# The end of a large matmul: leaving the last bank to the end and summing it in two halves

## Chip, cores and metric

One core of a Trainium2 chip. Kernels are compared only within the same rounds. The metric is the device time of one execution in microseconds (us), medians over several runs.

## The reference

```python
def setup_inputs():
    m, k, n = 4096, 4096, 4096
    return {
        "a": np.random.randn(m, k).astype(np.float32),
        "b": np.random.randn(k, n).astype(np.float32),
        "alpha": np.float32(0.01),
    }

def reference(a, b, alpha):
    x = np.matmul(a, b)
    return np.where(x > 0, x, alpha * x)
```

## The kernel before

The kernel works in bf16. It goes through the output in regions of 512 rows by 1024 columns: four row blocks (`mt`) times two column halves (`nt`), which are eight sums of 128 x 512 fp32, one in each of the eight PSUM banks. k is passed in four quarters (`u`) of eight steps of 128 (`c`). The parts that the change touches:

```python
    psum_pool = ctx.enter_context(tc.tile_pool(name="psum", bufs=8, space=bass.MemoryType.PSUM))
    o_pool = ctx.enter_context(tc.tile_pool(name="oo", bufs=2))
    # ... cut ...
    def mm(ps, mb, h, pi, u, mt, nt, c, first, last):
        rows = slice(mt * P, (mt + 1) * P)
        t = at[mb, h, u]
        nc.tensor.matmul(
            ps,
            plain(t)[:, c, rows] if (mb, h, u) == (0, 0, 0) else t[:, c // 2, rows, c % 2],
            bt[pi, u][:, c, nt * NT:(nt + 1) * NT],
            start=first,
            stop=last,
        )
    # ... cut: the first two regions, loads, transposes ...
    for r in range(HALVES, len(regions)):
        mb, h, pi, n = regions[r]
        banks = new_banks()
        final = r == len(regions) - 1
        for u in range(KU):
            last = u == KU - 1
            for mt in range(MT):
                if final and last:
                    todo = [(c, nt) for nt in range(NP) for c in range(KC)]
                else:
                    todo = [(c, nt) for c in range(KC) for nt in range(NP)]
                for c, nt in todo:
                    mm(banks[mt, nt], mb, h, pi, u, mt, nt, c, u == 0 and c == 0,
                       last and c == KC - 1)
                if last:
                    o = o_pool.tile([P, RN], FP32, name="o")
                    to = place(mb, h, n, mt)
                    for nt in range(NP):
                        cols = slice(nt * NT, (nt + 1) * NT)
                        nc.scalar.activation(o[:, cols], banks[mt, nt], LRELU, alpha=alpha)
                        if final and mt:
                            nc.sync.dma_start(to[:, cols], o[:, cols])
                    if not final or mt == 0:
                        nc.scalar.dma_start(to, o)
                # ... cut: loads for later regions ...
```

In the last region the two banks of a row block are finished one after the other, and each half of the block is stored as soon as its activation is done. What is left after the last matmul is one activation of 512 columns and one store of 256 KB.

Of the kernel before, what the change touches and what calls it, by code (L numbers as in the profile page):

```python
# [8 lines left out]
P = 128  # L9
BF16 = mybir.dt.bfloat16  # L10
FP32 = mybir.dt.float32
U32 = mybir.dt.uint32
LRELU = mybir.ActivationFunctionType.Lrelu
KC = 8

SEGS = [(0, 0, 8), (1, 0, 8), (2, 0, 8), (3, 0, 8)]
NT = 512
MT = 4
NP = 2
# [7 lines left out]
def kernel(  # L27
# [19 lines left out]
    nc = tc.nc  # L47
# [3 lines left out]
    alpha = float(alpha)  # L51

    KU = K // (KC * P)
# [15 lines left out]
    psum_pool = ctx.enter_context(tc.tile_pool(name="psum", bufs=8, space=bass.MemoryType.PSUM))  # L69
# [17 lines left out]
    bt = {}  # L87
# [59 lines left out]
    def plain(t):  # L147

        return t.rearrange("p c m e -> p (c m e)").rearrange("p (c m) -> p c m", c=KC)

    def mm(ps, mb, h, pi, u, mt, nt, c, first, last):
        rows = slice(mt * P, (mt + 1) * P)
        t = at[mb, h, u]
        nc.tensor.matmul(  # L154
            ps,
            plain(t)[:, c, rows] if (mb, h, u) == (0, 0, 0) else t[:, c // 2, rows, c % 2],
            bt[pi, u][:, c, nt * NT:(nt + 1) * NT],
            start=first,
            stop=last,
        )  # L160

    def new_banks():
        return {
            (mt, nt): psum_pool.tile([P, NT], FP32, name="ps")
            for mt in range(MT)
            for nt in range(NP)
        }

    def place(mb, h, n, mt):
        row = ((mb * HALVES + h) * MT + mt) * P  # L170
        return out[row:row + P, n * RN:(n + 1) * RN]
# [13 lines left out]
    for pi in range(1, len(pairs)):  # L185
        first = next(i for i, r in enumerate(regions) if r[2] == pi)
# [4 lines left out]
    for mb in range(1, MB):  # L191
        first = next(i for i, r in enumerate(regions) if r[0] == mb)
# [7 lines left out]
    def quarter_of(pieces, quarter):  # L200
        for piece in pieces[len(pieces) * quarter // 4:len(pieces) * (quarter + 1) // 4]:
            piece()
# [78 lines left out]
    banks = {}  # L281

    def work():
        for mt, c in waiting:
            for nt in range(NP):
                mm(banks[mt, nt], 0, 0, 0, 0, mt, nt, c, (mt, nt) not in begun, False)
                begun.add((mt, nt))
        waiting.clear()

    for n, (what, i) in enumerate(order):  # L290
# [4 lines left out]
        if n == 0:  # L295
            for _ in range(2):
                nc.tensor.matmul(wp, w[:, :P], w, start=True, stop=True)  # L297
            banks = new_banks()
# [18 lines left out]
    for nt in range(NP):  # L317
        for mt, c in waiting:
            mm(banks[mt, nt], 0, 0, 0, 0, mt, nt, c, False, True)
# [9 lines left out]
    for i in range(1, len(steps)):  # L329
        t, h, s, first, last = steps[i]  # L330
        u, c0, kc = SEGS[s]
# [17 lines left out]
        if first:  # L349
            banks = new_banks()  # L350
            if h not in part:
                part[h] = part_pool.tile([P, MT, RN], FP32, name="part", tag="part")
        for g, (todo, leaves) in enumerate(groups):
            for mt, c in todo:
                for nt in range(NP):
                    mm(banks[mt, nt], 0, h, 0, u, mt, nt, c0 + c, first and c == 0,
                       last and c == kc - 1)
            for piece, turn in enumerate(following):
                if where[piece] == g:
                    turn()  # L360
            if leaves is not None:
                spill(t, h, leaves, banks)
# [11 lines that stand above are left out]
                else:  # L374
                    todo = [(c, nt) for c in range(KC) for nt in range(NP)]
                for c, nt in todo:
                    mm(banks[mt, nt], mb, h, pi, u, mt, nt, c, u == 0 and c == 0,
                       last and c == KC - 1)
                if last:
                    o = o_pool.tile([P, RN], FP32, name="o")  # L380
                    to = place(mb, h, n, mt)
                    for nt in range(NP):
                        cols = slice(nt * NT, (nt + 1) * NT)
                        nc.scalar.activation(o[:, cols], banks[mt, nt], LRELU, alpha=alpha)  # L384
                        if final and mt:
                            nc.sync.dma_start(to[:, cols], o[:, cols])
                    if not final or mt == 0:
                        nc.scalar.dma_start(to, o)
                quarter_of(loads.get(r * KU + u, []), mt)


# [33 lines left out]
```

## Time and profile before

| quantity | value |
|---|---|
| time, median of 3 runs | 1785.11 us (1784.67 to 1785.48) |
| span of the profiled execution | 1783.2 us |
| TensorE busy | 99% of the span |
| start of the last activation | 1779.65 us |
| tail: from there to the end | 3.55 us |

"Tail" is used in this sense throughout. The prediction below shows the lines for all of this.

### The profile page before, as it was taken

What the parts mean: (1) busy time and instruction counts of PE and PEld (TensorE: products, weight loads), DVE (VectorE), ACT (ScalarE), POOL (GpSimd) and SP (SyncE); (2) the same over time, 40 slices, a digit from 0 to 9 for tenths busy, and PEclk for the clock granted to TensorE, in tenths of its full rate; (3) what the DMA queues carried; (4) which work ended last, traced back from release to release, by engine and by line L of the source; (5) the groups of instructions that cost most, each with busy time, mean ns of one, the idle gap of its engine ahead of it and who ended that gap; (6) DMA issues with size and microseconds to landing.
All of it is one profiled execution on the core that took longest, in us unless ns stands there. A gap on an engine that the chain in (4) does not pass through costs nothing.

```text
span 1783.2 us, 17975 instructions
## 1 busy us (share of the span) xinstructions
PE 1768.7 (99%) x8070; PEld 806.6 (45%) x8234; DVE 153.4 (9%) x117; ACT 152.0 (9%) x270; POOL 360.1 (20%) x663
## 2 busy tenths in 40 slices
PE   9999999999999999999999999999999999999999
PEld 4444444444444444444444444444444444444444
DVE  4530000032000000002200000000220000000000
ACT  2010000000000000000000000000000000000001
POOL 4630210433002020043201202014320110301000
PEclk9999999999999999999999999999999999999999
DMA  9994653987139165397704917449860481835511
GB/s 260 195 252 108 115 133 86 190 127 125 40 94 189 48 119 118 94 198 128 124 25 96 188 48 142 94 103 202 128 121 12 112 171 48 165 72 121 115 48 47
DMA packets 147020, 214.06 MB, mean 120 GB/s; under 512 B 12800, under 2 KB 76288, under 8 KB 146944
## 3 DMA queue, kind: packets, MB, share of 16 engines
q0 software_dynamic: 126208, 139.50, 48.3%
q10 hardware_dynamic: 18000, 65.54, 9.4%
q1 hardware_dynamic: 2736, 7.87, 1.2%
q8 instruction: 64, 1.05, 0.2%
q14 instruction: 12, 0.10, 0.0%
HBM read 285.21 MB, written 67.11 MB: 198 GB/s over the span
## 4 chain that ended last, share of the span: by engine, by line
PE 99%; issue 1%; DMA 0%; ACT 0%; SPq 0%; DVE 0%
PE ps L154 99%; DMA a_in<-in_a_dram 0%; PE turned L268 0%; DVE at L271 0%; ACT o L384 0%; ACT at L271 0%; SPq L253 0%; SPq L251 0%
## 5 line engine op out<-in xcount | busy, mean ns | idle before, releaser
L154 PE MATMUL ps<-bt,at 128*128 128x512 bf16 x8028 | 1760.5, 379 | 9.3 <-ACT bt L275 0.3
L154 PEld LDWEIGHTS <-at 128*128 128x128 bf16 x8192 | 801.4, 98 | 967.3 <-ACT at L271 1.3
L138 POOL DMA_DIRECT2D bt<-in_b_dram x408 | 217.1, 539 | 1084.7 <-PE ps L154 893.5
L384 ACT ACTIVATE o<-ps 128x512 f32<-128x512 f32 x240 | 130.7, 595 | 1524.5 <-PE ps L154 1450.8
L121 DVE STREAM_TRANSPOSE at<-a 128x1024 uint32<-128x1024 uint32 (+1 forms) x63 | 123.0, 1986 | 1135.7 <-PE ps L154 1113.8
L116 POOL DMA_DIRECT2D a<-in_a_dram x248 | 142.1, 579 | 203.4 <-DVE at L121 140.1
L231 DVE TENSOR_TENSOR part<-ps,part 128x512 f32<-128x512 f32 x32 | 20.4, 686 | 32.6 <-PE ps L154 32.6
L234 ACT ACTIVATE o<-part 128x1024 f32<-128x1024 f32 x8 | 8.5, 1057 | 77.0 <-DVE part L231 64.2
L229 ACT COPY part<-ps 128x512 f32<-128x512 f32 x8 | 4.4, 593 | 15.1 <-PE ps L154 12.3
L227 DVE COPY part<-ps 128x512 f32<-128x512 f32 x8 | 5.2, 679 | 4.8 <-PE ps L154 4.8
L268 PEld LDWEIGHTS turned<-ident,a_in 128*128 128x128 f32 x32 | 4.3, 196 | 2.4 <-issue 1.2
L268 PE MATMUL turned<-ident,a_in 128*128 128x128 f32 x32 | 4.8, 296 | 0.4 <-DMA a_in<-in_a_dram 0.4
L275 ACT CAST bt<-b_in 128x512 bf16<-128x512 f32 x8 | 5.0, 619 | 2.2 <-DMA b_in<-in_b_dram 2.1
L84 PE MATMUL ps<-w 128*128 128x512 bf16 x8 | 3.6, 631 | 1.2 <-DVE x L80 1.2
L275 DVE CAST bt<-b_in 128x512 bf16<-128x512 f32 x8 | 3.4, 432 | 3.8 <-DMA b_in<-in_b_dram 3.8
L271 DVE CAST at<-turned 128x512 bf16<-128x512 f32 x4 | 2.8, 692 | 10.5 <-PE turned L268 10.5
L271 ACT CAST at<-turned 128x512 bf16<-128x512 f32 x4 | 2.3, 585 | 8.7 <-PE turned L268 8.7
L311 POOL CAST x<-bt 128x1 f32<-128x1 bf16 x1 | 0.3, 348 | 11.1 <-ACT bt L275 11.1
L84 PEld LDWEIGHTS <-w 128*128 128x128 bf16 x8 | 1.0, 140 | 2.8 <-issue 1.7
L81 ACT ACT_TABLE_LOAD x1 | 1.3, 1283 | 0.7 <-PEq L406 0.7
L297 PE MATMUL ps<-w 128*128 128x512 bf16 x2 | 0.6, 379 | 0.0
L78 DVE MEMSET w<- 128x256 uint32 x1 | 0.3, 272 | 0.9 <-PEq L406 0.9
(9 smaller groups left out, 1.4 us busy)
## 6 DMA issues: line engine op xcount, KB each, us to landing
bt<-in_b_dram POOLq DMA_DIRECT2D x408, 256.0 KB, 7.9
out_dram<-o ACTq DMA_DIRECT2D x125, 512.0 KB, 3.1
a<-in_a_dram POOLq DMA_DIRECT2D x248, 128.0 KB, 5.2
b_in<-in_b_dram SPq DMA_DIRECT2D x7, 512.0 KB, 10.0
a_in<-in_a_dram SPq DMA_DIRECT2D x4, 512.0 KB, 7.0
out_dram<-o SPq DMA_DIRECT2D x6, 256.0 KB, 2.0
b_in<-in_b_dram SPq DMA_DIRECT2D x2, 256.0 KB, 10.4
```

The lines of the kernel that those rows point to most:

```text
L84: nc.tensor.matmul(wp, w[:, :P], w, start=True, stop=True)
L116: nc.gpsimd.dma_start(to, src.rearrange("(g i) w -> i g w", i=32))
L121: nc.vector.transpose(dst.rearrange("p c m e -> p c (m e)").bitcast(U32) .rearrange("p c (g i) -> p g c i", i=32), held[0][:, 4 * t0:4 * t ...
L138: nc.gpsimd.dma_start(new_b(pi, u)[:, c0 + c, :], b_rows(n, s, c))
L154: nc.tensor.matmul(ps, plain(t)[:, c, rows] if (mb, h, u) == (0, 0, 0) else t[:, c // 2, rows, c % 2], bt[pi, u][:, c, nt * NT:(nt + 1) * NT],
L227: nc.vector.tensor_copy(kept, banks[mt, nt])
L231: nc.vector.tensor_add(kept, banks[mt, nt], kept)
L234: nc.scalar.activation(o, part[h][:, mt, :], LRELU, alpha=alpha)
L268: nc.tensor.transpose(turned[i, 2 * c // kc0][:, c % (kc0 // 2), :], cols[:, c, :], ident)
L271: copy(plain(a0)[:, c:c + kc0 // 2, i * P:(i + 1) * P], turned[i, half])
L275: copy(b0[:, i, columns(nt)], b_in[i][:, columns(nt)])
L384: nc.scalar.activation(o[:, cols], banks[mt, nt], LRELU, alpha=alpha)
```

## The change

The intent is to shorten the tail. Bank (3,1), the last of the last region, gets no matmul until all other banks are done. Then its 512 columns are summed over all of k in two parts of 256, each in a bank of its own. The activation and the store of the first part lie under the matmuls of the second, so only a 256-column activation and a 128 KB store are left at the end. Besides, row block 1 is stored by one transfer from ACT instead of two from SP.

```diff
-    def mm(ps, mb, h, pi, u, mt, nt, c, first, last):
+    def mm(ps, mb, h, pi, u, mt, nt, c, first, last, cols=None):
 ...
-            bt[pi, u][:, c, nt * NT:(nt + 1) * NT],
+            bt[pi, u][:, c, cols or slice(nt * NT, (nt + 1) * NT)],
 ...
                 for c, nt in todo:
+                    if final and (mt, nt) == (MT - 1, NP - 1):
+                        continue
                     mm(banks[mt, nt], ...)
                 if last:
                     ...
                     for nt in range(NP):
+                        if final and (mt, nt) == (MT - 1, NP - 1):
+                            continue
                         ...
-                        if final and mt:
+                        if final and mt > 1:
                             nc.sync.dma_start(to[:, cols], o[:, cols])
-                    if not final or mt == 0:
+                    if not final or mt < 2:
                         nc.scalar.dma_start(to, o)
                 quarter_of(loads.get(r * KU + u, []), mt)
+        if final:
+            mt, nt = MT - 1, NP - 1
+            wide = NT // 2
+            for part_of in range(2):
+                cols = slice(nt * NT + part_of * wide, nt * NT + (part_of + 1) * wide)
+                ps = banks[mt, nt] if part_of == 0 else psum_pool.tile([P, NT], FP32, name="ps")
+                for u in range(KU):
+                    for c in range(KC):
+                        mm(ps[:, :wide], mb, h, pi, u, mt, nt, c, u == 0 and c == 0,
+                           u == KU - 1 and c == KC - 1, cols)
+                nc.scalar.activation(o[:, cols], ps[:, :wide], LRELU, alpha=alpha)
+                nc.sync.dma_start(to[:, cols], o[:, cols])
```

## The prediction

> **What bounds the kernel now.** I read the page first, then the chain of waits and the timeline of the last 20 us, because the change touches nothing but the last region. From the page of the kernel before (engine times; granted clock by slice; the chain that ended last; the two groups concerned; the last stores):
>
> ```profile
> span 1783.2 us, 17975 instructions
> PE 1768.7 (99%) x8070; PEld 806.6 (45%) x8234; DVE 153.4 (9%) x117; ACT 152.0 (9%) x270; POOL 360.1 (20%) x663
> ...
> PEclk9999999999999999999999999999999999999999
> ...
> PE ps L154 99%; DMA a_in<-in_a_dram 0%; PE turned L268 0%; DVE at L271 0%; ACT o L384 0%; ACT at L271 0%; SPq L253 0%; SPq L251 0%
> ...
> L154 PE MATMUL ps<-bt,at 128*128 128x512 bf16 x8028 | 1760.5, 379 | 9.3 <-ACT bt L275 0.3
> ...
> L384 ACT ACTIVATE o<-ps 128x512 f32<-128x512 f32 x240 | 130.7, 595 | 1524.5 <-PE ps L154 1450.8
> ...
> out_dram<-o SPq DMA_DIRECT2D x6, 256.0 KB, 2.0
> ```
>
> TensorE is busy 99% of the span at the full clock, and 99% of the chain is the one matmul line. All other engines wait for it: ACT's idle time at L384 is nearly all "<-PE". So the kernel is bound by the number of matmul columns times the column rate, plus a short start and a short tail. The change keeps the number of columns; only the tail, where TensorE has finished and the result has still to leave, can give time back. The timeline of the last microseconds (start, length, what) shows that tail:
>
> ```profile
> 1776.20 0.60 ACT L384 ACTIVATE o<-ps 128x512 f32<-128x512 f32 x1 [1.13 <-PE ps L154]
> 1777.97 0.60 ACT L384 ACTIVATE o<-ps 128x512 f32<-128x512 f32 x1 [1.18 <-PE ps L154]
> 1779.65 0.60 ACT L384 ACTIVATE o<-ps 128x512 f32<-128x512 f32 x1 [1.08 <-PE ps L154]
> ```
>
> ```profile
> 1780.28 0.33 SPq L386 DMA_DIRECT2D out_dram<-o  x1
> ```
>
> The last sum is complete at 1779.65; one 512-column activation (0.60 us) makes the last half row-block ready; the store is issued at 1780.28 and, by the median of its row, lands 2.0 us later at about 1782.28; the program then needs about 0.92 us to its end at 1783.2. The tail is 3.55 us of 1783.2, which is **0.2%**. No possible gain there reaches 2%. The reported time, 1785.11 us, lies 1.9 us above the profiled span; I take that difference as constant.
>
> Where within those 2.0 us the bytes move is seen in the DMA view of 1780.2 to 1783.2, 40 slices of 0.075 us:
>
> ```profile
> GB/s 0 0 0 0 0 0 0 0 0 0 0 0 273 328 437 410 437 355 410 328 355 164 0 0 0 0 0 0 0 0 0 0 0 0 0 0 0 0 0 0
> ```
>
> Data flow from about 1781.10 to 1781.83: some 0.73 us for 256 KB. The other 1.27 us before and after do not look as if they depend on the size.
>
> **What the Trainium skill says.** (1) "TensorE: Matmul & The Clock Gate", section "Back-to-back issue gap", gives N/2.4 + 2.5 ns for one warm matmul after another, 216 ns at N = 512. The trace agrees: evictions of consecutive banks start at 1771.02 and 1779.65 with five banks of eight matmuls between, 8.63 us / 40 = 215.75 ns. (The same section's 131 ns for a sustained N = 512 stream is not what this trace shows.) (2) The same page, section "LDWEIGHTS (loading the stationary operand)", gives 128/1.2 = 107 ns for a load of 128 columns; the trace has 98 ns and overlaps it. This is the number that matters for halves, which last about as long. (3) "ScalarE: Activation LUTs", section "What ACT_TABLE_LOAD costs", gives 186 ns + 0.833 ns per column, 612 ns at 512; the trace has 595 to 597. (4) "PSUM — Partial Sum Buffer", section "PSUM bank collisions raise a hardware error", says two engines must not touch one bank at one time, even in different columns. That is why each part has a bank of its own; no view of this kernel tests it.
>
> **The change part by part.**
>
> *Removed and moved.* Bank (3,1) loses its 4 x 8 = 32 matmuls of 512 columns inside the region. The 24 of the first three k quarters take 24 x 215.75 ns = 5.18 us, so all other banks of the region finish 5.18 us earlier: the eviction of bank (3,0) moves from 1777.97 to about 1772.8. These evictions lay under matmuls and still do, so this gives nothing.
>
> *Added.* 64 matmuls of 256 columns, each with its own weight load, in place of 32 with 32. With the fixed part taken from the measured spacing, 215.75 - 512/2.4 = 2.42 ns, one half matmul is 256/2.4 + 2.42 = 109.1 ns (an estimate). 64 x 109.1 = 6.98 us against 32 x 215.75 = 6.90 us: **+0.08 us** on the path, provided that a weight load hides behind 109 ns. TensorE ends at about 1779.73, and part 0 is complete one half earlier, at 1776.24.
>
> *The weight load, checked.* At 98 ns it fits, with 11 ns to spare. There is one stream of short matmuls in the trace, the eight fp32 transposes near the start (weight loads of 196 ns each on record), at full clock:
>
> ```profile
> 13.62 1.05 PE L268 MATMUL turned<-ident,a_in 128*128 128x128 f32 x8
> ...
> 14.51 0.81 PE L154 MATMUL ps<-bt,at 128*128 128x512 bf16 x3
> ```
>
> Start to start this is 0.89 us / 8 = 111 ns for a pair, though the load alone is listed at 196 ns; the earlier group (10.49 to 11.46) gives 121 ns. So a pair can be fed about every 111 ns, and the listed duration of a load is more latency than occupancy. A bf16 pair with half that listed duration should not be slower than 109 ns by much.
>
> *The tail.* The last activation has 256 columns instead of 512. With 0.833 ns per column it is 597 - 213 = 384 ns: **-0.21 us**. The last store has 128 KB instead of 256 KB, in 1 KB rows. At the same rate its data take 0.73/2 = 0.365 us: **-0.365 us**. The fixed 1.27 us and the 0.92 us after landing remain. Part 0's activation (1776.24 to 1776.62) and its store (issued 1776.65, landed by about 1778.3) lie under part 1's matmuls.
>
> *The other store.* Row block 1 goes out in one 512 KB store from ACT instead of two from SP. Its bank is evicted by about 1768.2 and, with the 2.7 us of that row in this window, it has landed by about 1770.9; row block 3, which reuses the output buffer, needs it at 1772.8. There are 1.9 us to spare: nothing.
>
> *Sum:* +0.08 - 0.21 - 0.365 = **-0.50 us**. The span would be 1782.7, the time 1784.6 us.
>
> **The rivals.** *A: the weight loads or instruction feed become the bound of the last 7 us.* There are now two instructions per 109 ns, and 98 ns of 109 is a thin margin. If a pair needs 121 ns as in the slower transpose group, the cost is 64 x 12 = +0.76 us and the net +0.26: 1785.4. If it needs 131 ns, 64 x 22 = +1.4 us and the net +0.9: 1786.0. For it: the thin margin. Against it: the 111 ns above, from loads with twice the listed duration. I give it one chance in four.
>
> *B: the store's time hardly depends on its size.* Smaller rows may move less efficiently, so that 128 KB take as long as 256 KB. Then only the activation counts: -0.13 us, 1785.0. Against it is the GB/s row, where data fill a third of the landing time. One in five, perhaps in part.
>
> *C: the second half waits for a bank.* The extra tile takes the oldest of eight banks, that of (0,0), whose eviction starts near 1767.57 - 5.18 = 1762.4; the second part needs it at 1776.24, some 13 us later. If instead it waited for part 0's eviction, the hole would be 0.4 us or so and the net about -0.1: 1785.0. Unlikely.
>
> **Range and chances.** The mechanisms span 1784.6 to 1786.0, leaning to the low end. The three runs before spread over 0.8 us (1784.67 to 1785.48), more than the expected effect, so that run-to-run scatter sets half of the range. I predict 1784.6 us with 1783.8 to 1785.8. Two per cent would be 36 us, ten times the whole tail; 99% for within 2%.
>
> **What the trace after would show.** Last activation 256 columns wide at 0.38 us; last store 128 KB landing in about 1.6 us; evictions of parts 0 and 1 about 3.49 us apart (32 x 109.1 ns), which is the test of A: 3.9 us would mean 121 ns a pair, 4.2 us 131 ns. TensorE without a wait between the parts tests C; a 2.0 us landing would show B. From the last activation's start to the end of the span: about 2.97 us instead of 3.55. I would be wrong if the halves run at well above 109 ns, or if the new program shifts the other 1770 us by more than the scatter, which nothing in the diff would do.

## More of the kernel before

One more line of the trace before will be needed, from ACT's timeline near the start (columns: start in us, length in us, engine, line, operation, what it works on, how many):

```profile
23.85 2.05 ACT L229 COPY part<-ps 128x512 f32<-128x512 f32 x4 [3.78 <-PE ps L154]
```

This is the first copy of a finished bank out of PSUM. Everything before it is the start of the program, where TensorE waits for the first loads. It serves as a mark behind the start.

## The result

The changed kernel took 1784.76 us (median of 6 runs, 1784.30 to 1785.16). In the same rounds the kernel before took 1785.20 us (6 runs, 1784.67 to 1785.49). The ratio of the times is 0.9997, with a 95% interval of 0.9985 to 1.0010. Ratios here are the mean time of one kernel's fast runs over that of the other's of the same rounds, so not quite the ratio of the quoted medians. The medians differ by 0.44 us and the means by 0.46 us.

From the page of the changed kernel (the span; the group of the last two activations; the stores by size, with the median time from issue to landing):

```profile
span 1782.5 us, 18202 instructions
...
L405 ACT ACTIVATE o<-ps 128x256 f32<-128x256 f32 x2 | 0.8, 384 | 6.0 <-PE ps L154 6.0
...
out_dram<-o SPq DMA_DIRECT2D x3, 256.0 KB, 2.0
...
out_dram<-o SPq DMA_DIRECT2D x2, 128.0 KB, 1.7
```

The timeline of its last microseconds (columns as above):

```profile
1772.46 0.60 ACT L388 ACTIVATE o<-ps 128x512 f32<-128x512 f32 x1 [1.13 <-PE ps L154]
1775.95 0.38 ACT L405 ACTIVATE o<-ps 128x256 f32<-128x256 f32 x1 [2.90 <-PE ps L154]
1776.36 3.83 SPq L406 DMA_DIRECT2D out_dram<-o  x2
1779.45 0.38 ACT L405 ACTIVATE o<-ps 128x256 f32<-128x256 f32 x1 [3.11 <-PE ps L154]
```

And its bytes moved, 1779.5 to 1782.5 in 40 slices of 0.075 us:

```profile
GB/s 0 0 0 0 0 0 0 0 0 0 0 0 0 0 0 41 232 369 341 328 314 109 14 0 0 0 0 0 0 0 0 0 0 0 0 0 0 0 0 0
```

Read it from the top. The evictions of bank (3,0) and of the two parts start at 1772.46, 1775.95 and 1779.45. The two parts are 3.50 us apart, which is 109 ns for each matmul with its weight load. The activations take 384 ns. The SPq row (SPq is SyncE's own queue of instructions, from which these stores are issued) spans two issues, from 1776.36 to 1780.19; an issue takes 0.33 us, so the last store is issued at 1779.86. From there to the end at 1782.5 it is 2.64 us, against 2.92 us before (1780.28 to 1783.2). The tail is 1782.5 - 1779.45 = 3.05 us, against 3.55.

The span is shorter by 0.7 us and the tail by 0.50. The rest is not the change. The mark behind the start, in the changed kernel's trace:

```profile
23.57 2.05 ACT L229 COPY part<-ps 128x512 f32<-128x512 f32 x4 [3.51 <-PE ps L154]
```

It lies 0.28 us earlier than before (23.85), in code that both kernels share. From this mark to the last activation it is 1779.65 - 23.85 = 1755.80 us before and 1779.45 - 23.57 = 1755.88 us after. So the span closes: -0.28 at the start (chance), +0.08 in the matmuls, -0.50 in the tail, together -0.70.

This is the measure for what follows. Over all profiles the mark falls anywhere between 23.28 and 24.34 us. The way from the mark to the last activation, on the other hand, repeats to 0.01 us in the three kernels that were profiled twice (changed, quarters, 384 and 128). One profile, that of e4, has a delay just behind the mark; it is told there. From mark to end the kernel before takes 1759.35 us and the changed one 1758.93 us: **-0.42 us**, beside -0.46 us in the means of the times.

### The profile page after: what moved, and what is told of

Read it like the earlier page. It is cut to its first block, busy times and chain, and to the rows that moved or that the text cites. A ratio compares the mean times of both kernels' runs of the same rounds, so it can differ in the third digit from the quotient of the medians.

```text
span 1782.5 us, 18202 instructions
## 1 busy us (share of the span) xinstructions
PE 1777.3 (100%) x8266; PEld 809.5 (45%) x8266; DVE 153.5 (9%) x117; ACT 152.1 (9%) x271; POOL 360.4 (20%) x663
## 4 chain that ended last, share of the span: by engine, by line
PE 99%; DMA 0%; ACT 0%; SPq 0%; DVE 0%; issue 0%
PE ps L154 99%; DMA a_in<-in_a_dram 0%; PE turned L268 0%; DVE at L271 0%; ACT at L271 0%; SPq L253 0%; ACT o L405 0%; SPq L251 0%
```

## The experiments

All outputs are right. The first table gives for each kernel its last store and the numbers from its trace. "Issue to end" runs from the issue of the last store. The end is known to 0.1 us. The column "completion semaphore" is explained under experiments 6 and 11.

| kernel | last store, KB | completion semaphore | mark to last activation | tail | issue to end | mark to end |
|---|---|---|---|---|---|---|
| before | 256 | 8th | 1755.80 | 3.55 | 2.92 | 1759.35 |
| changed | 128 | 8th | 1755.88 | 3.05 | 2.64 | 1758.93 |
| e1: one part | 256 | 7th | 1755.80 | 3.57 | 2.95 | 1759.37 |
| e2: quarters | 64 | 2nd | 1756.04 | 3.14 | 2.83 | 1759.18 |
| e3: 384, 128 | 64 | 8th | 1755.88 | 2.78 | 2.47 | 1758.66 |
| e4: one store | 256 | 7th | 1756.22 | 3.42 | 3.01 | 1759.64 |
| e5: same bank | 128 | 8th | 1756.52 | 3.04 | 2.63 | 1759.56 |
| e6: row block 1 from SP | 128 | 1st | 1755.88 | 3.54 | 3.12 | 1759.42 |
| e7: changed, again | 128 | 8th | 1755.88 | 3.10 | 2.68 | 1758.98 |
| e8: 448, 64 | 32 | 8th | 1755.88 | 2.68 | 2.43 | 1758.56 |
| e9: 384, 128, again | 64 | 8th | 1755.88 | 2.76 | 2.46 | 1758.64 |
| e10: quarters, again | 64 | 2nd | 1756.04 | 3.14 | 2.83 | 1759.18 |
| e11: one store more | 128 | 1st | 1755.88 | 3.45 | 3.04 | 1759.33 |
| e12: quarters, six stores more | 64 | 8th | 1756.04 | 2.76 | 2.45 | 1758.80 |

The second gives the times: the median, and the difference of the mean from that of the kernel before in the same rounds, beside the difference from mark to end in the trace.

| kernel | runs | time, median us | mean against before | trace against before |
|---|---|---|---|---|
| changed | 6 | 1784.76 | -0.46 | -0.42 |
| e7: changed, again | 5 | 1784.88 | -0.43 | -0.37 |
| e1 | 5 | 1785.11 | +0.10 | +0.02 |
| e2 | 5 | 1784.61 | -0.55 | -0.17 |
| e3 | 5 | 1784.24 | -0.83 | -0.69 |
| e9 | 5 | 1784.48 | -0.83 | -0.71 |
| e4 | 5 | 1785.04 | +0.02 | +0.29 (-0.05 without a delay at the start) |
| e5 | 5 | 1785.56 | +0.22 | +0.21 |
| e8 | 5 | 1784.75 | -0.60 | -0.79 |
| e6 | 4 | 1784.65 | -0.38 | +0.07 |
| e11 | 5 | 1784.81 | -0.33 | -0.02 |
| e12 | 5 | 1784.88 | -0.43 | -0.55 |

Every ratio's interval is 0.12 to 0.17% wide on either side, over 2 us, so none of these times is different from before. e10 was one look and took 1785.18 us.

### e1: the order alone

```diff
-            wide = NT // 2
-            for part_of in range(2):
-                cols = slice(nt * NT + part_of * wide, nt * NT + (part_of + 1) * wide)
+            at_col = 0
+            for part_of, wide in enumerate([512]):
+                cols = slice(nt * NT + at_col, nt * NT + at_col + wide)
+                at_col += wide
```

The same loop, with other widths, makes the parts of e2, e3 and e8; their edits are shown below without the lines of `at_col`.

> The last bank is left to the end and summed over all of k, but in one part of 512 columns with one activation and one 256 KB store. Theory (the gain comes only from the smaller last activation and the smaller last store): nothing is gained; from the start of the last activation to the end of the span 3.55 us as before, time within 0.3 us of before (about 1785.2). Rival (the gain comes from the order, because the stores of the other banks have long drained when the last one goes out): the tail is about 3.05 us as in the changed kernel, and the time about 1784.7.

From its timeline, bank (3,0) and the one last part:

```profile
1772.82 0.60 ACT L388 ACTIVATE o<-ps 128x512 f32<-128x512 f32 x1 [1.13 <-PE ps L154]
...
1779.73 0.60 ACT L406 ACTIVATE o<-ps 128x512 f32<-128x512 f32 x1 [6.31 <-PE ps L154]
```

The span was 1783.3 us, the tail 3.57 us. The 32 matmuls of the last bank take 6.91 us. Mark to end is that of before within 0.02 us, and so is the time within its scatter. Leaving the bank to the end gains nothing; the rival falls. The gain comes from the split.

### e4: two parts, one store

```diff
                 nc.scalar.activation(o[:, cols], ps[:, :wide], LRELU, alpha=alpha)
-                nc.sync.dma_start(to[:, cols], o[:, cols])
+            cols = slice(nt * NT, (nt + 1) * NT)
+            nc.sync.dma_start(to[:, cols], o[:, cols])
```

> The changed kernel, but both parts of the last bank leave in one store of 256 KB after the second activation. Theory (activation 0.21 us, store size some 0.25 to 0.37 us of the gain): the tail is 3.3 to 3.4 us, time about 1785.0. Rival 1 (the store's time does not depend on its size): tail 3.05 us as in the changed kernel, time 1784.7. Rival 2 (all from the store): tail 3.55 us.

From its timeline, the last activation and the store:

```profile
1780.28 0.38 ACT L405 ACTIVATE o<-ps 128x256 f32<-128x256 f32 x1 [3.11 <-PE ps L154]
1780.69 0.33 SPq L407 DMA_DIRECT2D out_dram<-o  x1
```

With the span of 1783.7 the tail is 3.42 us: 0.15 less than e1, whose last store has the same size and the same semaphore, and 0.37 more than the changed kernel, of which about 0.06 us may be one place in the turn of the semaphores (7th for 8th, see e6). So both terms are there, and the store's is the larger.

This profile also had 0.34 us more between the mark and the last activation. They were lost just behind the mark, in the start. From its timeline, the mark, a wait of TensorE for a VectorE transpose that the changed kernel's profile does not list, and the next copy:

```profile
24.06 2.06 ACT L229 COPY part<-ps 128x512 f32<-128x512 f32 x4 [3.69 <-PE ps L154]
25.70 6.65 PE L154 MATMUL ps<-bt,at 128*128 128x512 bf16 x30 [0.16 <-DVE at L121]
29.19 0.59 ACT L229 COPY part<-ps 128x512 f32<-128x512 f32 x1 [3.07 <-issue]
```

From the mark to that copy it is 5.13 us, in the changed kernel 4.79 (23.57 to 28.36). From the copy to the last activation it is 1751.09 us in both. So the mark lay a little too early to take off the whole start. Without the 0.34 us, e4 lies 0.05 us below before in the trace, which fits its time; the tail is not touched by it.

### e2 and e10: quarters

```diff
-            wide = NT // 2
-            for part_of in range(2):
+            for part_of, wide in enumerate([128, 128, 128, 128]):
 ... cut: at_col, as in e1 ...
```

> The last bank in four parts of 128 columns, each in its own bank: 128 matmuls of 128 columns. The hidden weight load of the halves is put to the test. If the load keeps hiding, a pair takes 55.8 ns, the parts are evicted 1.79 us apart, and with a tail of some 2.8 us (activation 277 ns, store 64 KB) the time is about 1784.6. If a load occupies its listed 98 ns, the parts are 3.14 us apart, 5.4 us are added, and the time is about 1790.0; if a pair costs the 111 ns of the fp32 transposes, 3.55 us apart and about 1791.7.

The four evictions of e2:

```profile
1774.31 0.28 ACT L406 ACTIVATE o<-ps 128x128 f32<-128x128 f32 x1 [1.19 <-PE ps L154]
...
1776.09 0.28 ACT L406 ACTIVATE o<-ps 128x128 f32<-128x128 f32 x1 [1.51 <-PE ps L154]
1777.88 0.28 ACT L406 ACTIVATE o<-ps 128x128 f32<-128x128 f32 x1 [1.51 <-PE ps L154]
1779.66 0.28 ACT L406 ACTIVATE o<-ps 128x128 f32<-128x128 f32 x1 [1.51 <-PE ps L154]
```

Three parts of 32 pairs take 5.35 us, 55.7 ns for a matmul of 128 columns and its weight load, although the trace still lists 98 ns for each load. The load is hidden far better than the listed duration suggests: rival A of the prediction falls, with a wide margin. The whole costs 0.24 us more than one part (1756.04 against 1755.80).

But the tail was 3.14 us, where about 2.8 had been expected, and the issue to end was 2.83 us.

> The quarters again, for one more profile: from the issue of the last 64 KB store to the end of the span the first profile had 2.83 us, where the 384 and 128 kernel with the same last store had 2.46 and 2.47. If that was scatter of the end of the program, 2.4 to 2.6 us now; if four stores in a row cost something at the end, 2.8 us again.

It gave 3.14 and 2.83 again, so this was not scatter. It stayed open until e12.

### e3 and e9: 384 and 128 columns

```diff
-            wide = NT // 2
-            for part_of in range(2):
+            for part_of, wide in enumerate([384, 128]):
 ... cut: at_col, as in e1 ...
```

> The last bank in a part of 384 and one of 128 columns. Theory with hidden loads: the second part takes 1.79 us, total matmul time +0.08 us over before, tail 2.8 us, time about 1784.5, 0.2 below the changed kernel. With 98 ns a load: second part 3.14 us, +1.4 us, time about 1785.9, slower than before. With about 65 ns a pair (in between): second part 2.1 us, time about 1784.8, no better than two halves.

The evictions of its two parts:

```profile
1777.43 0.49 ACT L406 ACTIVATE o<-ps 128x384 f32<-128x384 f32 x1 [4.60 <-PE ps L154]
...
1779.22 0.28 ACT L406 ACTIVATE o<-ps 128x128 f32<-128x128 f32 x1 [1.29 <-PE ps L154]
```

The second part takes 1.79 us, 56 ns a pair. The matmuls cost the same 0.08 us as the two halves do, since only the number of matmuls counts. The tail is 2.78 us. The time, 1784.24, was the lowest so far.

> 384 and 128 columns again, beside the changed kernel on the same chip. Theory (a shorter last part costs no matmul time, its activation saves 0.11 us more and its 64 KB store some 0.1 us more): 0.2 us below the changed kernel, about 1784.5, 0.6 below before. Rival (the 1784.24 of the first time was a lucky draw): no different from the changed kernel.

1784.48 us, and again 0.83 us below before in the mean; mark to end within 0.02 us of the first. The changed kernel, on the same chip in the same rounds, was 0.43 below. This is the version of choice: 0.7 us below before and 0.3 below the changed kernel in the trace.

### e7: the changed kernel again

No edit.

> The changed kernel again, unaltered, for the scatter of the tail and of the time. If the gain is the one worked out from the traces so far (matmuls +0.08, activation -0.21, store -0.2 us), it is 0.3 to 0.5 us below before: 1784.7 to 1784.9. If the first comparison was scatter, the two times agree within 0.15 us. Evictions of the two parts 3.50 us apart again; from the last activation's start to the end 3.05 to 3.2 us.

1784.88 us, 0.43 us below before in the mean (0.46 the first time). Its tail is 3.10 us and mark to end 1758.98. The profiled span was 1783.0 and not 1782.5, since the mark lay at 24.02.

### e8: 448 and 64 columns

```diff
-            wide = NT // 2
-            for part_of in range(2):
+            for part_of, wide in enumerate([448, 64]):
 ... cut: at_col, as in e1 ...
```

> 448 and 64 columns: how far does a weight load hide? At 64/2.4 + 2.4 = 29 ns a pair the second part would take 0.93 us. If a load of 128 columns needs about 54 ns of the array (the 55.7 ns of the quarters would then be its limit as much as the matmul's), it takes about 1.75 us and adds 0.8 us: about 1785.1, no better than before. If everything hides: about 1784.4.

From its timeline, and then from its groups by shape:

```profile
1779.29 0.54 ACT L406 ACTIVATE o<-ps 128x448 f32<-128x448 f32 x1 [5.46 <-PE ps L154]
...
1780.22 0.22 ACT L406 ACTIVATE o<-ps 128x64 f32<-128x64 f32 x1 [0.39 <-PE ps L154]
```

```profile
L154 PE MATMUL ps<-bt,at 128*128 128x64 bf16 x32 | 1.1, 193 | 0.0
```

0.93 us for 32 pairs: 29 ns each, and no idle time. Even here the loads hide, at least for a run of 32. The tail is 2.68 us, only 0.09 less than with 128 columns: issue to end falls by 0.03 us or so and the activation by 0.05. The 224 KB store of the first part is issued only 0.6 us before the last one, and their data follow each other without a gap. The time does not tell it from e9.

### e5: both parts in one bank

```diff
-                ps = banks[mt, nt] if part_of == 0 else psum_pool.tile([P, NT], FP32, name="ps")
+                ps = banks[mt, nt]
```

> The changed kernel, but both parts in the one bank (3,1), so that the second part must wait until the first has been evicted: what a bank of its own is worth. TensorE waits between the parts for the activation of 0.38 us and the way of the semaphores, 0.5 us in all or a little more; the evictions of the parts are 4.0 us apart instead of 3.50; time about 1785.3, the whole gain lost. If the wait were hidden, 3.50 us and 1784.8.

From its timeline, the first eviction, the matmuls of the second part with the idle time ahead of them, and the second eviction:

```profile
1776.33 0.38 ACT L405 ACTIVATE o<-ps 128x256 f32<-128x256 f32 x1 [2.90 <-PE ps L154]
...
1776.77 3.65 PE L154 MATMUL ps<-bt,at 128*128 128x256 bf16 x32 [0.47 <-ACT o L405]
1780.46 0.38 ACT L405 ACTIVATE o<-ps 128x256 f32<-128x256 f32 x1 [3.74 <-PE ps L154]
```

TensorE stands still for 0.47 us until ACT has emptied the bank. The evictions are 4.13 us apart instead of 3.50. That costs 0.63 us; the 0.16 us beyond the wait pass after the restart, and why is not shown. The cost is more than the split gains, and the mean of the times points the same way: +0.22 us, though within the interval. The bank of its own is what makes the split worth while.

### e6, e11, e12: which semaphore the last store takes

e6 undoes the third part of the change:

```diff
-                        if final and mt > 1:
+                        if final and mt:
                             nc.sync.dma_start(to[:, cols], o[:, cols])
-                    if not final or mt < 2:
+                    if not final or mt == 0:
                         nc.scalar.dma_start(to, o)
```

> The changed kernel with its third part undone: row block 1 again leaves in two stores from SP and not in one from ACT. Theory (these stores are hidden some 10 us before the end): evictions and tail as in the changed kernel (3.50 us apart; 3.0 to 3.1 us from the last activation's start to the end), time 1784.8 within the scatter of 0.3 us. Rival (the move matters for the last stores or for a buffer): the eviction of bank (3,0) or the tail shifts by more than 0.1 us.

The matmuls and the evictions were as expected, the tail was not. Its last eviction, with a span of 1782.7:

```profile
1779.16 0.38 ACT L405 ACTIVATE o<-ps 128x256 f32<-128x256 f32 x1 [3.11 <-PE ps L154]
```

The tail is 3.54 us, as long as before the change, and issue to end is 3.12 us instead of 2.64, though the last store has the same 128 KB. In the trace the move of row block 1's store is worth half a microsecond.

The compiled program tells why it may be. In it the stores from SP and ACT use eight completion semaphores in turn, DMAHW0 to DMAHW7 (a completion semaphore is a counter by which a store reports that it has landed); a store first waits for the last user of the one it takes. The last two stores of the changed kernel and of e6, from the list of SyncE's instructions:

```text
changed: 17 L406 DMACopy out_dram<-o 128x256 [waits DMAHW6_49,Activation_49]
         18 L406 DMACopy out_dram<-o 128x256 [waits DMAHW7_49,Activation_49]
e6:      19 L406 DMACopy out_dram<-o 128x256 [waits DMAHW7_49,Activation_49]
         20 L406 DMACopy out_dram<-o 128x256 [waits DMAHW0_49,Activation_49]
```

For row block 1, e6 has two stores from SP where the changed kernel has one from ACT. It issues one store more, and the last one moves on from the eighth semaphore to the first. At the end of the program SyncE waits for semaphores one after the other. From the trace, its semaphore instructions at the end (count, shortest/median/longest in ns, first and last start in us), in two windows of the changed kernel:

```profile
L437 SPq EVENT_SEMAPHORE  x8: 28/28/28, 1780.2 to 1780.7; - x8
...
L437 SPq EVENT_SEMAPHORE  x1: 28/28/28, 1781.6 to 1781.6; - x1
```

and in one window of e6:

```profile
L437 SPq EVENT_SEMAPHORE  x8: 27/28/28, 1781.3 to 1781.8; - x8
```

In the changed kernel eight are done while the last store is under way, and one is left when it lands. In e6 one comes before (at 1780.0) and these eight after the landing. This fits the compiled programs: after the last store SyncE has one other wait, then those for DMAHW0 to DMAHW7 in this order. A last store on the first semaphore leaves all the others behind it. Two experiments test that, in both directions. e11 is the changed kernel with row block 0's store, far from the end, split into two:

```diff
-                        nc.scalar.dma_start(to, o)
+                        if final and mt == 0:
+                            for piece in range(2):
+                                span = slice(piece * (RN // 2), (piece + 1) * (RN // 2))
+                                nc.scalar.dma_start(to[:, span], o[:, span])
+                        else:
+                            nc.scalar.dma_start(to, o)
```

> The changed kernel, but row block 0 of the last region leaves in two stores instead of one, some 12 us before the end: one store more, so that the last store of all takes the first of the eight completion semaphores in turn instead of the eighth. Theory (the program ends by waiting for the eight in order, and each wait that is still to do after the last store has landed costs some 0.06 us): from the issue of the last store to the end about 3.1 us instead of 2.65, tail 3.5 us instead of 3.05, time about 1785.2, the gain of the change lost. Rival (the 3.12 us seen with row block 1 from SP came from the five stores on that queue, or was scatter): 2.65 us, tail 3.05 us, time 1784.8.

e12 is the quarters, with row blocks 0 and 1 in four stores each, which brings the last store from the second semaphore to the eighth.

```diff
-                        nc.scalar.dma_start(to, o)
+                        if final:
+                            for piece in range(4):
+                                span = slice(piece * (RN // 4), (piece + 1) * (RN // 4))
+                                nc.scalar.dma_start(to[:, span], o[:, span])
+                        else:
+                            nc.scalar.dma_start(to, o)
```

> The quarters, with row blocks 0 and 1 in four stores each: six stores more, so that the last one takes the eighth semaphore instead of the second. Theory: from the issue of the last 64 KB store to the end 2.47 us instead of 2.83, tail 2.75 to 2.8 us instead of 3.14. Matmuls +0.23 us, so the time is some 0.55 us below before: about 1784.6, a little above the 384 and 128 kernel. Rival (four small stores in a row are slow to complete): 2.83 us and 3.14 us again.

The end of e11 (its span is 1782.9 us), first the last eviction, then the semaphore instructions after the landing:

```profile
1779.45 0.38 ACT L410 ACTIVATE o<-ps 128x256 f32<-128x256 f32 x1 [3.11 <-PE ps L154]
```

```profile
L442 SPq EVENT_SEMAPHORE  x8: 28/28/28, 1781.6 to 1782.0; - x8
```

And the last eviction of e12 (its span is 1783.0 us):

```profile
1780.24 0.28 ACT L411 ACTIVATE o<-ps 128x128 f32<-128x128 f32 x1 [1.51 <-PE ps L154]
```

In the traces the theory holds in both directions: extra stores far from the end move the last store's place, and with it the end, by 0.4 us. e11's last activation starts at 1779.45, to the hundredth where the changed kernel's does, and the program ends 0.4 us later; eight waits follow the landing again. e12's tail is 2.76 us instead of 3.14, and its issue to end 2.45 us, as with the same store in e3 and e9. Seven waits more cost 0.40 and 0.48 us (e11, e6), six 0.37 us (e2): about 0.06 us each.

**What stays open:** the times do not show it. e6 and e11 should have lost the gain, but lie 0.38 and 0.33 us below before, and e2 lies 0.38 further below than its trace says. In the profiled run itself the waits are in the time: for e6, 23.28 + 1759.42 us make its span of 1782.7, and its time was 1784.45, 1.75 more (1.74 to 1.89 in all runs). The start's scatter may hide them (the marks of the profiles of e6, e11 and e2, 23.28, 23.57 and 23.62, are among the early ones), or the waits at the end may be cheaper in runs other than the profiled one. Chance is not a comfortable answer, because time and trace differ by 0.31 to 0.45 us in just the three kernels that end on the first or second semaphore and by less than 0.2 us in all others (e4 without its delay). Four or five runs each, with no trace of the others, don't decide it. So the cost of the waits is shown for profiled executions only.

## Why the prediction was right

The predicted time was 1784.6 us; 1784.76 was measured, in the range. By its steps:

- **Bound by the matmul columns, only the tail to win: right.** From the mark to the last activation the two kernels differ by 0.08 us in 1756.
- **+0.08 us for 64 half matmuls: right.** 6.99 us (1772.46 to 1779.45) against 6.91 us in e1. The fixed part of 2.4 ns per matmul also gives the quarters (+0.24 us) and the unequal parts (+0.08).
- **The weight load hides behind 109 ns: right, and the doubt was too large.** Rival A had one chance in four. Loads hide behind 55.7 ns (e2), and behind 29 ns for 32 pairs (e8).
- **-0.21 us for the activation: right.** 597 to 384 ns.
- **-0.365 us for the store: the mis-sized term.** The step took the same rate for half the data. From issue to end it measured 2.92 to 2.64 us, and 2.68 in e7: -0.24 to -0.28 us. In the GB/s rows the data take about 0.5 us for 128 KB, against 0.73 us for 256 KB: the full slices in the middle carry 314 to 369 GB/s, against 328 to 437 before, and the slices at the ends, which carry less, are as many as before or more. The sum is +0.08 - 0.21 - 0.26 = -0.39 us instead of -0.50; measured -0.42 and -0.37 in the traces.
- **Rival B, the store's time hardly depends on its size: wrong as put, true in part.** Issue to end is 2.92, 2.64, 2.46 and 2.43 us for 256, 128, 64 and 32 KB, all on the eighth semaphore, so that the trend flattens (the data of the 32 KB follow straight on those of another store). And the rate did fall with the 1 KB rows, as B feared; whether by the rows or by the size of the transfer, no run separates.
- **Rival C, a wait for the bank: did not occur.** e5 shows what it would cost: 0.63 us, where the prediction had put 0.4; the change would then have been slower in the trace, not 0.1 us faster.
- **Row block 1's store gains nothing: wrong in the traces.** The argument looked only at buffers and at when the store lands. It missed that the number of stores sets the last store's place among the completion semaphores: the split adds a store, and the move takes one away. Had the change kept two stores there, the profiled tail would have been 3.5 us (e6). Because before and after both end on the eighth semaphore, the sum came out right without this step; that was luck.
- **Run-to-run scatter sets half of the range: right.** Its place is mostly the start: the mark moves by 1.06 us over the profiles. (The 1.9 us between time and span set a median against the span of another run; the profiled run's own time, 1784.97, is 1.8 us above its span. The sum is not touched by this.)

## What to carry to other kernels

After the last matmul, only the last piece's eviction and store count. Make that piece narrow and leave the piece before it wide: two parts of 384 and 128 columns cost as little matmul time as two halves and end earlier, as long as each part has its own bank. For differences below a microsecond, subtract the scattered start by a mark in the trace; here this made a number that repeats to 0.05 us out of times that scatter by 1 us. Set the mark behind the last wait of the start: in one profile here 0.34 us were lost between the mark and the next copy. And when a store is added or removed anywhere, look in the profile at the waits at the program's end before explaining the tail by the store's size.

## What the Trainium skill lacked or had wrong

- "TensorE: Matmul & The Clock Gate", section "Back-to-back issue gap": its sustained spacings of a matmul with its weight load, 131 ns at 512 columns and 81 ns at 128, are not what these runs show: 215.75 and 55.7 ns, and 109 ns at 256. Its other formula, N/2.4 + 2.5 ns, which it calls the isolated one, fits all of them, down to 29 ns at 64 columns (32 pairs).
- The same page, section "LDWEIGHTS (loading the stationary operand)": 128/1.2 = 107 ns. The traces list 98 ns. As a limit on the rate of loads, which this section alone might suggest, neither holds here: 128 loads in a row were fed at 55.7 ns each and 32 at 29 ns.
- "ScalarE: Activation LUTs", section "What ACT_TABLE_LOAD costs": 186 ns + 0.833 ns per column. The slope fits; the constant here is 171 ns (597, 491, 384, 277 and 224 ns at 512, 384, 256, 128 and 64 columns).
- "DMA: Bandwidth & Descriptors", section "Anatomy of one DMA — SWDGE (gpsimd) path", fits a fixed 2.0 us plus the size for transfers issued from GpSimd. For small stores issued from SP the page has no such fit; issue to landing was 2.0, 1.7 to 1.8, 1.5 to 1.6 and 1.5 us for 256, 128, 64 and 32 KB.
- No page was found that has the waits for the stores at the end of the program itself: SyncE waits for the eight completion semaphores one after the other, some 0.06 us each in profiled executions, so that the place of the last store in the turn is worth up to 0.48 us (not seen in the times).
